# Three reorderings around PE's waits in a two-layer decoder trunk: key copies, memory products, one chunk's split

## The chip, the cores and the metric

The kernel runs on one core of one Trainium2 chip. The metric is the device time of one execution in microseconds (us); runs are compared by their median. PE is the matmul engine (PEld its weight loads), DVE the vector engine, ACT the scalar engine, POOL the GpSimd engine, and SP the engine whose queue issues most of the DMAs.

## The reference

A residual stream of 256 tokens of width 1024 passes two layers. Each layer has a token mixer with memory cross-attention beside it, a layer norm, a large product-key expert layer (PEER), and a second layer norm. Layer 0's mixer is an mLSTM, layer 1's an RG-LRU.

```
for i in range(2):
    z = x @ w_in[i]                                   # mixer streams and 4 cross-attention query heads
    hm = mlstm_mixer(z) if i == 0 else rglru_mixer(z)
    ha = cross_attention(xq, mem, xattn_w_kv[i])       # kv = mem @ w_kv; softmax over 256 memory tokens
    mix = concat([hm, ha]) @ w_out[i]
    x = layer_norm(ALPHA * x + mix, ln1_g[i], ln1_b[i])
    y = peer_ffn(x, peer_w_q[i], peer_subkeys[i], peer_u[i], peer_v[i])   # top 16 of 16384 experts, 8 heads
    x = layer_norm(ALPHA * x + y, ln2_g[i], ln2_b[i])
```

## The kernel before

Everything is computed in float32 quality with three matmuls for one product. A number is split into a high part, rounded to the fast matmul format (`wH`, `xH`, `memH`), and the remainder (`wL`, `xL`, `memL`); `mm3` (lines 182 to 186) multiplies high by high, high by low and low by high. Weights come from memory in chunks of 128 rows by up to 1024 columns. The program is written out by hand in one order for all engines, and each engine works off its own queue in that order.

**The ring of chunks.** `plan` lists every chunk in the order of use. `load` (L139) issues the DMA of a chunk on SP's queue into one of five buffers `raw`. `pump` splits it: a cast on ACT makes `wH` (L110), and a subtraction makes `wL`, either on DVE (L125), on POOL (L123), or with the first `pool_cols` columns on POOL and the rest on DVE. The rest can be put off (`put_off`): then it is kept in the list `owed` and issued later. A raw buffer is free when all readers are done. `next` hands out the next chunk; it pumps up to three chunks ahead (`HL_BUFS`), and first lets a side generator take a step.

**Side generators.** `beside(gen)` registers work that is issued in small steps, one step at each call of `next`. In layer 0's mixer, `gates` (L592) is such a generator: it computes the gates of the mLSTM on [4, 256] tiles on ACT and DVE, and copies the projected keys from PSUM into `kT` on ACT with `keys(t0, t1)` (L645). Its steps run while the projection of the queries goes on, whose chunks (`w0qx`) alternate with four parts of the transposed memory (`memT`, cast on ACT to `memH`, subtracted on POOL to `memL`).

**Layer norm.** `norm` (L284) is a generator that lets the caller issue matmuls at each of its `yield`s. It has two halves of tokens, tt = 0 and 1. `add` and `half` (L303 to L311) add the residual and take statistics, `stats` (L315, L316) finishes them, `center` (L324) and `spread` (L329) scale a stretch of 256 or 512 columns, `scale` does both, `scale_beside` (L336 to L340) does it on ACT and POOL. `turn(tt, q, n)` transposes a stretch of the result on PE (L350), casts it on ACT into `xH` (L354) and subtracts on DVE into `xL` (L355), the operands of the next projection. `idle` (L249) puts transposes of the identity into PE's queue.

- *Behind the token mixer* (`early`): `proj_n` with a `tail` calls it. In layer 0 the tail is 6 chunks, in layer 1 all 8 (`tail == DT`). After `g` and `b`, the norm's weights, the ring holds the first chunks of the query projection `w_q`. The norm pumps the first of them with its `wL` wholly on POOL, and the next, with 512 columns on POOL and 512 put off, between the first and second statistics of tt = 1. Later it scales the first two blocks of tt = 1 on DVE (L425), transposes them (L428), casts them (L429), subtracts (L432), issues what was put off, and scales the next quarter (`scale(1, 1, 1)`). The rest of the scaling and turning goes into the generator `rest`, which steps at each `next` of the following projection: `scale(0, 2, 2)` and `turn(1, 1, 1)`, then `scale(1, 2, 2)` and `turn(0, 2, 2)`, then `turn(1, 2, 2)`. That projection belongs to `peer_layer`, which first clears 16 small tiles on POOL (L1093, L1094).
- *Behind layer 0's experts* (`fill`): the caller passes a generator `memory` with six steps of products that do not depend on the norm, four of `mem_k` and two of `mem_v` (12 matmuls each), for the cross-attention of layer 1. The norm takes some of them before, between and after its turns, so that PE has work while DVE scales.

The steps of `memory` in the order before:

```
next(fill), next(fill)
turn(0, 0, 1), turn(1, 0, 1)
scale(0, 2, 2)
owed.pop()()
next(fill)
turn(0, 1, 1), turn(1, 1, 1)
scale(1, 2, 2)
next(fill), next(fill)
turn(0, 2, 2)
next(fill)
turn(1, 2, 2)
```

Of the kernel before, what the change touches and what calls it, by code (L numbers as in the profile page):

```python
# [19 lines left out]
D = 1024  # L20
T = 256
DT = 8
# [12 lines left out]
MIX_COLS = 0  # L35
# [15 lines left out]
class Trunk:  # L51
# [98 lines left out]
    def next(self, ahead=HL_BUFS):  # L150
        while callable(self.items[self.n_got][2]) or self.items[self.n_got][3] is not None:
            self.pump(self.n_got + 1)
            self.split.pop(self.n_got, None)
            self.n_got += 1
        i = self.n_got
        if self.ahead:
            next(self.ahead, None)
        self.pump(i + ahead)
        self.n_got += 1
        self.tick()  # L160
        return self.split.pop(i)
# [37 lines left out]
    def proj_n(self, splits, stat, order=range(DT), tail=0, extra=EXTRA, hook=(-1, None)):  # L199
        sH, sL = stat  # L200
        parts = [splits, (512, 256, 256) if tail else splits]
        banks = [[self.bank() for _ in p] for p in parts]
        late = []

        def products(tt, k, late):
            t = slice(tt * P, (tt + 1) * P)
            w = parts[tt][k]
            c0 = sum(parts[tt][:k])
            for n_, dt_, (h, l) in late:
                self.mm3(banks[tt][k][:, :w], sH[:, dt_, t], sL[:, dt_, t], h[:, c0:c0 + w], l[:, c0:c0 + w],  # L210
                         n_ == 0, n_ == last[tt])
        n_ring = DT - 2 - extra
        last = (DT - 1, DT - 1 - n_ring if tail else DT - 1)
        for n, dt in enumerate(order):
            if n == hook[0]:
                hook[1]()
            late.append((n, dt, self.next(min(HL_BUFS + min(n, extra), DT - n) if tail else HL_BUFS)))
            if n + 1 > DT - tail and n + 1 < DT:
                continue
            if tail and n + 1 == DT:  # L220
                break
            for tt in range(2):
                for k in range(len(parts[tt])):
                    products(tt, k, late)
            late = []
        if not tail:
            return banks
        ln = self.norm(banks, False, True)
        if tail == DT:
            own, ring = late[2:2 + extra], late[:2] + late[2 + extra:]  # L230
            parts0 = [[c] for c in late]
        else:
            parts0 = own, ring = late[:-n_ring], late[-n_ring:]
        for n, part in enumerate(parts0):
            if tail == DT and n == 2:
                self.idle(FILL[2])
            for k in range(2):
                products(0, k, part)
        next(ln)
        for k in range(3):  # L240
            products(1, k, ring)
        for k in range(3):
            products(1, k, own), next(ln, None)
# [37 lines left out]
        tmp.__exit__(None, None, None)  # L281


    def norm(self, y, last, early, fill=False):  # L284
        nc, x = self.nc, self.x
        alpha = 1.0 if last or fill else ALPHA
        fine = early or last
# [18 lines left out]
        def half(tt, q0, n):  # L306
            if fine and tt:
                for q in range(q0, q0 + n):
                    nc.vector.bn_stats(st[:, tt, q, :], x[:, tt, q * Q:(q + 1) * Q])
            else:  # L310
                nc.vector.bn_stats(st[:, tt, q0 // 2, :], x[:, tt, q0 * Q:(q0 + 2) * Q])  # L311
# [9 lines left out]
        def center(tt, q, n):  # L321
            qs = slice(q * Q, (q + n) * Q)
            xs = x[:, tt, qs]
            nc.vector.scalar_tensor_tensor(xs, xs, mv[:, tt, 0:1], g[:, qs], op0=ALU.subtract, op1=ALU.mult)  # L324
# [61 lines left out]
            part = add(1, 0)  # L386
        half(*part)
        owed = []
        if early:
            self.pool_cols = D  # L390
            self.pump(self.n_got + 3)
        self.pool_cols, self.put_off = 512, owed.append
        self.pump(self.n_got + 3 + early)
        self.put_off = None
        self.pool_cols = MIX_COLS
        yield
        half(*add(1, 1))
        yield
# [4 lines left out]
        if fill:  # L403
            center(1, 0, 1), root(1), spread(1, 0, 1)
            scale(1, 1, 1)
            next(fill), next(fill)
            turn(0, 0, 1), turn(1, 0, 1)
            scale(0, 2, 2)
            owed.pop()()
            next(fill)  # L410
            turn(0, 1, 1), turn(1, 1, 1)
            scale(1, 2, 2)
            next(fill), next(fill)
            turn(0, 2, 2)
            next(fill)
            turn(1, 2, 2)
            self.release("g", "b")
            yield
            return
# [10 lines left out]
        low()  # L430
        for dt in range(2):
            nc.vector.tensor_sub(self.xL[:, dt, P:], ps[dt][:, :P], self.xH[:, dt, P:].bitcast(F32))  # L432
        self.idle(FILL[1])
        owed.pop()()
        scale(1, 1, 1)
# [116 lines left out]
    def mlstm_layer(self):  # L552
        nc, tc, A = self.nc, self.tc, self.A
        with ExitStack() as ctx:
# [37 lines left out]
            def gates():  # L592
                ig, fg = g2[:, 0, :], g2[:, 1, :]
                ab, e, wv, ln, F, lf = (gt[:, i, :] for i in range(6))
                nc.scalar.activation(fg, kg[3][32:36, :T], AF.Identity, bias=bg[:, 1:2])
                nc.scalar.activation(ig, kg[3][0:4, :T], AF.Identity, bias=bg[:, 0:1])
                nc.vector.scalar_tensor_tensor(ab, fg, -1.0, fg, op0=ALU.mult, op1=ALU.min)
                nc.vector.scalar_tensor_tensor(ab6, lam, -1.0, lam, op0=ALU.mult, op1=ALU.min)
                keys(0, 1)
                yield  # L600
                nc.scalar.activation(e, ab, AF.Exp)
                nc.scalar.activation(e6, ab6, AF.Exp)
                nc.vector.tensor_scalar(wv, e, 1.0, None, op0=ALU.add)
                nc.vector.tensor_scalar(w6, e6, 1.0, None, op0=ALU.add)
                nc.vector.memset(ab, 1.0)
                keys(1, 2)
                yield
                nc.scalar.activation(ln, wv, AF.Ln)
                nc.scalar.activation(l6, w6, AF.Ln)
                nc.vector.scalar_tensor_tensor(wv, wv, -1.0, e, op0=ALU.add, op1=ALU.subtract)  # L610
                keys(2, 4)
                yield
                nc.vector.scalar_tensor_tensor(lf, fg, 0.0, ln, op0=ALU.min, op1=ALU.subtract)
                nc.vector.tensor_add(lf, lf, wv)
                keys(4, 6)
                yield
                nc.vector.tensor_tensor_scan(F, ab, lf, 0.0, op0=ALU.mult, op1=ALU.add)
                yield
                nc.vector.tensor_sub(rt[0:4, :], ig, F)
                nc.vector.tensor_tensor_scan(M, rt[0:4, :], rt[0:4, :], 0.0, op0=ALU.max, op1=ALU.max)  # L620
                yield
                nc.vector.tensor_add(ab, F, M)
                nc.vector.tensor_copy(rt[32:36, :], ab)
                nc.vector.tensor_scalar(M, M, -1.0, None, op0=ALU.mult)
                yield
                nc.scalar.dma_start(row, M)
                nc.vector.scalar_tensor_tensor(w6, w6, -1.0, e6, op0=ALU.add, op1=ALU.subtract)
                nc.vector.tensor_sub(l6, l6, w6)
                nc.vector.tensor_scalar(ab6, lam, -1.0, 0.0, op0=ALU.mult, op1=ALU.max)
                nc.vector.tensor_add(l6, ab6, l6)  # L630
                nc.vector.tensor_scalar(n8, l6, 8.0, None, op0=ALU.mult)
                nc.vector.tensor_scalar(c8, l6, -8.0, None, op0=ALU.mult)
                yield
                every = lambda n, o: bass.AP(tensor=row.tensor, offset=row.offset + o, ap=[[0, P], [T, 4], [1, n]])
                nc.scalar.dma_start(pw[:, :, 0:T], every(T, 0))
                nc.scalar.dma_start(pw[:, :, T:384], every(P, P))
                diag = bass.AP(tensor=pw.tensor, offset=pw.offset, ap=[pw.ap[0], [384, 4], [T, 2], [1, P]])
                nc.gpsimd.tensor_tensor(diag, diag, maskn.unsqueeze(1).unsqueeze(1).to_broadcast([P, 4, 2, P]),
                                        op=ALU.add)

            def keys(t0, t1):
                for tl in range(t0, t1):
                    src = kg[tl // 2][:, (tl % 2) * T:(tl % 2 + 1) * T]
                    for h, part, rows in KMAP[tl]:
                        nc.scalar.activation(kT[rows, h, part, :], src[rows], AF.Copy, scale=192.0 ** -0.5)  # L645
# [43 lines left out]
            for h in range(4):  # L689
                n = self.bank()  # L690
# [838 lines left out]
```

## Time and profile before

| | us |
|---|---|
| median of 3 runs | 1803.55 |
| lowest and highest | 1802.96 and 1803.71 |
| the profiled execution | 1803.17 |
| its span | 1801.4 |
| PE, DVE, ACT, POOL busy in it | 1785.8, 1489.8, 1012.4, 427.0 |

The span runs from the first to the last instruction of the profiled execution. All starts in the profile's rows are in us from the start of the span. A row of a timeline gives the start, the duration, engine, line, operation, result and operands with their sizes, how many instructions it stands for (xN), and in brackets the idle time ahead of it and what ended that. Matmuls overlap, so that a matmul of 0.28 us is followed by the next one much sooner. A row of waits names the waiting instruction, what released it, the total, the number of waits and the longest.

### The profile page before, as it was taken

Reading aid. Unit: us, or ns where it says so; the run is one execution under the profiler, and the core shown is the slowest. Engines: PE = TensorE matmul, PEld = TensorE weight load, DVE = VectorE, ACT = ScalarE, POOL = GpSimd, SP = SyncE. Lnnn points to the kernel's source line nnn. Section 1 sums busy time; section 2 is a strip of 40 time slices with the busy share of each in tenths; the row PEclk is TensorE's granted clock in tenths of the full one; section 3 lists DMA queues with packets and bytes.
Section 4 is the critical chain, followed back from the end, with each engine's and each line's share of the span. In section 5 each row is a group of like instructions: output and inputs, shape, how many; then the busy total and the mean of one; then the engine's idle time right before and its main releaser. Section 6 shows DMA issues by size and latency. Waiting matters only on the chain.

```text
span 1801.4 us, 33797 instructions
## 1 busy us (share of the span) xinstructions
PE 1785.8 (99%) x12717; PEld 1648.6 (92%) x12717; DVE 1489.8 (83%) x3091; ACT 1012.4 (56%) x1786; POOL 427.0 (24%) x324
## 2 busy tenths in 40 slices
PE   8999999999999999999999999999999999999998
PEld 8999999999999888888899899999999988888886
DVE  6674779599998899998867848685999989999987
ACT  6554555455554666665647355554555456666663
POOL 2015772333332000000101368325333300000000
PEclk9999999999999999999999999999999999999999
DMA  7656566655555566655755455665555556555664
GB/s 249 202 161 197 169 195 192 193 171 165 163 160 160 190 206 210 208 200 182 255 184 182 131 176 178 197 191 187 164 161 159 162 188 204 193 194 194 207 200 139
DMA packets 95557, 334.24 MB, mean 186 GB/s; under 512 B 10652, under 2 KB 13728, under 8 KB 95136
## 3 DMA queue, kind: packets, MB, share of 16 engines
q1 hardware_dynamic: 93752, 328.93, 56.7%
q10 hardware_dynamic: 1640, 3.15, 0.5%
q8 instruction: 99, 1.62, 0.4%
q14 instruction: 66, 0.54, 0.1%
HBM read 330.98 MB, written 1.05 MB: 184 GB/s over the span
## 4 chain that ended last, share of the span: by engine, by line
PE 74%; issue 16%; POOL 7%; DVE 2%; ACT 1%; DMA 0%; POOLq 0%; SPq 0%; DVEq 0%
PE bank L186 24%; PE bank L185 24%; PE bank L184 23%; POOL wL L120 7%; PE bank L256 3%; ACT wH L110 0%; DVE wL L125 0%; PE bank L350 0%; POOL wL L123 0%; PE bank L527 0%; DVE x L324 0%; PE bank L249 0%; DMA cp<-in_rg_par_dram 0%; DVE x L303 0%; DMA raw<-in_w0kg_dram 0%
## 5 line engine op out<-in xcount | busy, mean ns | idle before, releaser
L110 ACT CAST wH<-raw 128x1024 fp32r<-128x1024 f32 (+3 forms) x605 | 612.5, 1013 | 664.8 <-POOL wL L120 187.6
L184 PE MATMUL bank<-xHL,wH 128*128 128x256 f32 x2536 | 715.5, 282 | 4.6 <-ACT wH L110 4.6
L186 PE MATMUL bank<-xHL,wL 128*128 128x256 f32 x2536 | 702.5, 277 | 0.5 <-DVE wL L125 0.5
L185 PE MATMUL bank<-xHL,wH 128*128 128x256 f32 x2536 | 702.5, 277 | 0.0
L125 DVE TENSOR_TENSOR wL<-raw,wH 128x1024 fp32r<-128x1024 f32 (+3 forms) x413 | 449.5, 1090 | 227.3 <-ACT wH L110 226.4
L184 PEld LDWEIGHTS bank<-xHL,wH 128*128 128x128 f32 x2536 | 477.2, 188 | 4.7 <-ACT wH L110 4.6
L186 PEld LDWEIGHTS bank<-xHL,wL 128*128 128x128 f32 x2536 | 477.0, 188 | 1.1 <-DVE wL L125 0.7
L185 PEld LDWEIGHTS bank<-xHL,wH 128*128 128x128 f32 x2536 | 477.7, 188 | 0.1
L185 PE MATMUL bank<-wL,cH 128*128 128x512 f32 x850 | 331.1, 390 | 0.4 <-DVE wL L125 0.4
L186 PE MATMUL bank<-wH,cL 128*128 128x512 f32 x850 | 330.7, 389 | 0.0
L184 PE MATMUL bank<-wH,cH 128*128 128x512 f32 x850 | 330.3, 389 | 0.0
L123 POOL TENSOR_TENSOR wL<-raw,wH 128x1024 fp32r<-128x1024 f32 (+1 forms) x121 | 253.5, 2098 | 210.1 <-ACT wH L110 209.2
L120 POOL TENSOR_TENSOR wL<-raw,wH 128x386 fp32r<-128x386 f32 x126 | 129.5, 1028 | 280.1 <-DVE wL L118 280.1
L185 PEld LDWEIGHTS bank<-wL,cH 128*128 128x128 f32 x850 | 159.5, 188 | 34.8 <-DVE wL L125 1.3
L184 PEld LDWEIGHTS bank<-wH,cH 128*128 128x128 f32 x850 | 159.6, 188 | 33.7
L186 PEld LDWEIGHTS bank<-wH,cL 128*128 128x128 f32 x850 | 159.6, 188 | 33.6
L1036 DVE TENSOR_TENSOR oh<-iota,i12T 128x1024 f16<-128x1024 f16 x128 | 130.6, 1020 | 0.0
L339 POOL TENSOR_TENSOR x<-x,raw 128x256 f32<-128x256 f32 x6 | 5.0, 826 | 466.4 <-ACT x L336 466.4
L118 DVE TENSOR_TENSOR wL<-raw,wH 128x640 fp32r<-128x640 f32 x126 | 104.0, 825 | 7.5
L1039 DVE TENSOR_TENSOR oh<-oh,gT 128x1024 f16<-128x1024 f16 x128 | 90.1, 704 | 4.4
L1169 PE MATMUL bank<-oh 128*128 128x128 f16 x1024 | 80.9, 220 | 1.1 <-DVE oh L1039 1.1
L1169 PEld LDWEIGHTS <-oh 128*128 128x128 f16 x1024 | 58.8, 97 | 6.0 <-DVE oh L1039 1.5
(336 smaller groups left out, 2134.2 us busy)
## 6 DMA issues: line engine op xcount, KB each, us to landing
raw<-in_u_dram SPq DMA_DIRECT2D x256, 512.0 KB, 3.5
raw<-in_v_dram SPq DMA_DIRECT2D x256, 512.0 KB, 4.4
raw<-in_w_q_dram SPq DMA_DIRECT2D x32, 512.0 KB, 3.7
raw<-in_w_out_dram SPq DMA_DIRECT2D x16, 512.0 KB, 3.7
raw<-in_w0qx_dram SPq DMA_DIRECT2D x8, 512.0 KB, 5.1
raw<-in_wkv_dram SPq DMA_DIRECT2D x8, 512.0 KB, 5.1
raw<-in_w0v_dram SPq DMA_DIRECT2D x8, 384.0 KB, 5.0
raw<-in_w0o_dram SPq DMA_DIRECT2D x8, 384.0 KB, 3.0
```

Source lines behind the costliest of these rows:

```text
L110: (nc.vector.tensor_copy if self.cast_dve else nc.scalar.copy)(h[:, c], r[:, c])
L118: nc.vector.tensor_sub(l[:, k:], r[:, k:], h[:, k:].bitcast(F32))
L120: nc.gpsimd.tensor_sub(l[:, :k], r[:, :k], h[:, :k].bitcast(F32))
L123: nc.gpsimd.tensor_sub(l[:, :k], r[:, :k], h[:, :k].bitcast(F32))
L125: rest = lambda l=l, r=r, h=h, c=slice(k, n): nc.vector.tensor_sub(l[:, c], r[:, c], h[:, c].bitcast(F32))
L184: mm(out, sH, mH, start=start, stop=False, skip_group_check=True)
L185: mm(out, sH, mL, start=False, stop=False, skip_group_check=True)
L186: mm(out, sL, mH, start=False, stop=stop, skip_group_check=True)
L256: self.nc.tensor.matmul(out, lhsT, rhs, start=start, stop=stop, skip_group_check=True)
L1036: nc.vector.tensor_tensor(flat(oh[:, 1:3]), self.iota2.unsqueeze(1).to_broadcast([P, 4, P, 2]), pairs(self.i12T[:, j]), op=ALU.is_equal)
L1039: nc.vector.tensor_tensor(flat(oh[:, 0:2]), two.rearrange("p z (q e t) -> p z q e t", q=2, t=2), pairs(self.gT[:, j]), op=ALU.mult)
L1169: nc.tensor.matmul(wp[:, qs], oh[:, 2, q // 2, :, q % 2], oh[:, z, q // 2, :, q % 2], start=z == 0, stop=z == 1, skip_group_check=True)
```

## The change

Three moves, and no instruction more or less:

1. In `gates`, `keys(2, 4)` moves from the third step to the fourth, and `keys(4, 6)` from the fourth to the fifth. In ACT's queue each of the two groups of copies now stands one memory part and one weight chunk later.
2. In the norm behind layer 0's experts, three steps of `memory` come ahead of the first turns instead of two, and one fewer comes behind `scale(1, 2, 2)`. In PE's queue the third part of `mem_k` stands before the first four transposes, the fourth before the next four, and the first of `mem_v` alone before the four after them.
3. In layer 1's norm behind the mixer, the split of the second `w_q` chunk (the fourth item of the ring, counted with `g` and `b`) is issued behind the first casts and subtractions of tt = 1. In ACT's queue its cast moves from before the first turn to behind the L429 casts. In the queues of DVE and POOL the order stays: POOL's half still stands ahead of the 16 clears, DVE's half still behind L432. The three lines that set and reset `pool_cols` and `put_off` become a helper, `ahead`, for both norms behind a mixer.

```
-        ln = self.norm(banks, False, True)
+        ln = self.norm(banks, False, True, late=tail == DT)
...
-    def norm(self, y, last, early, fill=False):
+    def norm(self, y, last, early, fill=False, late=False):
...
         owed = []
+
+        def ahead(n, cols):
+            self.pool_cols, self.put_off = cols, owed.append
+            self.pump(self.n_got + n)
+            self.put_off = None
+            self.pool_cols = MIX_COLS
         if early:
-            self.pool_cols = D
-            self.pump(self.n_got + 3)
-        self.pool_cols, self.put_off = 512, owed.append
-        self.pump(self.n_got + 3 + early)
-        self.put_off = None
-        self.pool_cols = MIX_COLS
+            ahead(3, D)
+        if not late:
+            ahead(3 + early, 512)
         yield
...
-            next(fill), next(fill)
+            next(fill), next(fill), next(fill)
             turn(0, 0, 1), turn(1, 0, 1)
             scale(0, 2, 2)
             owed.pop()()
             next(fill)
             turn(0, 1, 1), turn(1, 1, 1)
             scale(1, 2, 2)
-            next(fill), next(fill)
+            next(fill)
             turn(0, 2, 2)
...
             nc.vector.tensor_sub(self.xL[:, dt, P:], ps[dt][:, :P], self.xH[:, dt, P:].bitcast(F32))
+        if late:
+            ahead(3 + early, 512)
         self.idle(FILL[1])
         owed.pop()()
         scale(1, 1, 1)
...
                 nc.vector.scalar_tensor_tensor(wv, wv, -1.0, e, op0=ALU.add, op1=ALU.subtract)
-                keys(2, 4)
                 yield
                 nc.vector.scalar_tensor_tensor(lf, fg, 0.0, ln, op0=ALU.min, op1=ALU.subtract)
                 nc.vector.tensor_add(lf, lf, wv)
-                keys(4, 6)
+                keys(2, 4)
                 yield
                 nc.vector.tensor_tensor_scan(F, ab, lf, 0.0, op0=ALU.mult, op1=ALU.add)
+                keys(4, 6)
                 yield
```

## The prediction

> **What bounds the kernel now.** I read the page first, then the waits of PE, then, around each place where PE waits, the timelines of PE, ACT, DVE and POOL, and last those same stretches by DVE and POOL alone.
>
> ```profile
> span 1801.4 us, 33797 instructions
> ...
> PE 1785.8 (99%) x12717; PEld 1648.6 (92%) x12717; DVE 1489.8 (83%) x3091; ACT 1012.4 (56%) x1786; POOL 427.0 (24%) x324
> ```
>
> The whole list of what PE waited for is short. Three of its rows carry this change (total, times, longest, in us):
>
> ```profile
> PE bank L428 <- DVE x L425: 0.9, 2, 0.7
> PE bank L350 <- DVE x L329: 0.5, 1, 0.5
> PE bank L186 <- DVE wL L125: 0.5, 1, 0.5
> ```
>
> PE is busy in 99% of the span, so an edit that moves only ACT, DVE or POOL work can pay or cost where PE waits for them and nowhere else. Each edit aims at one of these waits: the key copies at the L186 one, the memory products at the L350 one, the later split at the longer of the two L428 ones. No instruction is added or dropped; all three are changes of order. So what is at stake is under 2.5 us of 1801.4, and the question for each edit is what is late next.
>
> **Edit 1, key copies two steps later (layer 0).** PE, ACT, DVE and POOL around the wait (start, duration):
>
> ```profile
> 36.81 0.28 PE L184 MATMUL bank<-xHL,wH 128*128 128x256 f32 x1
> 36.92 0.28 PE L185 MATMUL bank<-xHL,wH 128*128 128x256 f32 x1
> 37.74 0.38 PE L186 MATMUL bank<-xHL,wL 128*128 128x256 f32 x1 [0.55 <-DVE wL L125]
> ...
> 40.65 0.38 PE L186 MATMUL bank<-xHL,wL 128*128 128x256 f32 x1
> ```
>
> ```profile
> 34.05 0.66 ACT L645 ACTIVATE kT<-bank 128x256 f32<-128x256 f32 x2
> 34.59 0.62 ACT L110 CAST memH<-raw 128x512 fp32r<-128x512 f32 x1
> 35.10 1.06 ACT L110 CAST wH<-raw 128x1024 fp32r<-128x1024 f32 x1
> 36.06 1.16 ACT L645 ACTIVATE kT<-bank 64x256 f32<-64x256 f32 x3
> ```
>
> ```profile
> 35.30 1.31 POOL L123 TENSOR_TENSOR memL<-raw,memH 128x512 fp32r<-128x512 f32 x1 [5.08 <-ACT memH L110]
> 37.80 3.96 POOL L123 TENSOR_TENSOR memL<-raw,memH 128x512 fp32r<-128x512 f32 x2 [1.20 <-ACT memH L110]
> ```
>
> ```profile
> 36.20 1.49 DVE L125 TENSOR_TENSOR wL<-raw,wH 128x1024 fp32r<-128x1024 f32 x1 [1.81 <-ACT wH L110]
> 39.39 1.21 DVE L125 TENSOR_TENSOR wL<-raw,wH 128x1024 fp32r<-128x1024 f32 x1
> ```
>
> PE's L186 starts at 37.74, just behind the end of the wL subtraction (36.20 + 1.49 = 37.69). Without the wait it would follow L185 by one pitch of 0.11 us (36.81 to 36.92), at 37.03, so 0.71 us are lost. The subtraction took 1.49 us where its neighbour took 1.21: it stood still until POOL's memL subtraction ended (35.30 + 1.31 = 36.61) and then ran 1.08 us.
>
> With the two copies moved behind this chunk, the memH cast starts at 34.05 instead of 34.59, and POOL's memL, the wH cast and what follows move by the same 0.54. POOL ends at 36.07, wL at 36.07 + 1.08 = 37.15, L186 starts at 37.20: 0.54 gained, 0.17 of the wait left. What is late next is the following chunk. On ACT the copies come behind wH (35.52 to 36.18), then memH and wH of that chunk, the second of them ending near 37.7; its memL subtraction on POOL waits for DVE until 37.15 and ends near 38.3; the two small gate operations of DVE queued behind wL wait for that and end near 39.0; then wL runs 1.21, to 40.2. PE gets to that chunk's L186 at 37.20 + (40.65 - 37.74) = 40.1 and waits about 0.1 more. It starts at 40.2 instead of 40.65. **Edit 1 is worth 0.45 us**, between 0.2 and 0.7 (the whole wait). The loads queued on SP behind these buffers are released earlier, not later. The moved copies read banks that nobody wants back in these steps.
>
> **Edit 2, one more part of memory products (layer 0's last norm).** PE, then DVE, then POOL:
>
> ```profile
> 918.06 0.38 PE L350 MATMUL bank<-ident,x 128*128 128x128 f32 x2
> 918.92 0.44 PE L350 MATMUL bank<-ident,x 128*128 128x128 f32 x2 [0.48 <-DVE x L329]
> ...
> 925.84 0.60 PE L350 MATMUL bank<-ident,x 128*128 128x128 f32 x4
> ```
>
> ```profile
> 918.11 0.76 DVE L329 SCALAR_TENSOR_TENSOR x<-x,rs,raw 128x256 f32<-128x256 f32 x1
> 918.79 1.50 DVE L324 SCALAR_TENSOR_TENSOR x<-x,mv,raw 128x256 f32<-128x256 f32 x1
> ...
> 924.89 0.75 DVE L329 SCALAR_TENSOR_TENSOR x<-x,rs,raw 128x512 f32<-128x512 f32 x1
> ```
>
> ```profile
> 918.54 1.46 POOL L123 TENSOR_TENSOR wL<-raw,wH 128x512 fp32r<-128x512 f32 x1
> ```
>
> The second pair of transposes waits 0.64 us (918.92 less 918.06 and two pitches of 0.11) for L329, which ends at 918.87. Twelve products at that pitch (1.3 us) put in front cover that wait wholly. But DVE's order does not change, and DVE runs from there without a pause to the last L329 of this norm, 924.89 + 0.75 = 925.64, on which the last four transposes depend; they started at 925.84. PE arrives there 0.64 us sooner, at 925.20, and waits until 925.69 (the earlier pair started 0.05 behind its L329). So the wait mostly moves to the last transposes: **edit 2 is worth 0.15 us**, between 0 and the 0.64 that it would be if DVE were not the next bound.
>
> **Edit 3, the fourth chunk's split behind the first copies (layer 1's first norm).** PE; then the same DVE instruction in layer 0's norm and in this one; then POOL; then ACT:
>
> ```profile
> 1016.83 0.50 PE L428 MATMUL bank<-ident,x 128*128 128x128 f32 x2 [0.75 <-DVE x L425]
> ...
> 1020.62 0.38 PE L350 MATMUL bank<-ident,x 128*128 128x128 f32 x2
> ...
> 1026.85 0.60 PE L350 MATMUL bank<-ident,x 128*128 128x128 f32 x4
> ```
>
> ```profile
> 136.93 0.48 DVE L324 SCALAR_TENSOR_TENSOR x<-x,mv,raw 128x256 f32<-128x256 f32 x1
> ```
>
> ```profile
> 1015.15 1.07 DVE L324 SCALAR_TENSOR_TENSOR x<-x,mv,raw 128x256 f32<-128x256 f32 x1
> ...
> 1018.98 1.51 DVE L329 SCALAR_TENSOR_TENSOR x<-x,rs,raw 128x256 f32<-128x256 f32 x1
> ...
> 1022.99 1.45 DVE L125 TENSOR_TENSOR wL<-raw,wH 128x512 fp32r<-128x512 f32 x1
> ...
> 1025.14 0.75 DVE L329 SCALAR_TENSOR_TENSOR x<-x,rs,raw 128x512 f32<-128x512 f32 x1
> ...
> 1029.06 0.69 DVE L125 TENSOR_TENSOR wL<-raw,wH 128x512 fp32r<-128x512 f32 x1 [0.26 <-ACT wH L110]
> ```
>
> ```profile
> 1012.31 3.63 POOL L123 TENSOR_TENSOR wL<-raw,wH 128x1024 fp32r<-128x1024 f32 x2
> 1015.88 0.20 POOL L1093 MEMSET edge<- 128x128 f16 x1
> ...
> 1018.93 1.28 POOL L123 TENSOR_TENSOR wL<-raw,wH 128x512 fp32r<-128x512 f32 x1 [0.65 <-ACT wH L110]
> ...
> 1029.10 1.80 POOL L123 TENSOR_TENSOR wL<-raw,wH 128x512 fp32r<-128x512 f32 x1 [1.89 <-ACT wH L110]
> ```
>
> ```profile
> 1017.16 0.47 ACT L429 CAST xHL<-bank 128x128 fp32r<-128x128 f32 x2 [1.72 <-PE bank L428]
> ...
> 1017.80 1.05 ACT L110 CAST wH<-raw 128x1024 fp32r<-128x1024 f32 x1 [0.17 <-ACT xHL L429]
> ...
> 1024.79 1.05 ACT L110 CAST wH<-raw 128x1024 fp32r<-128x1024 f32 x1
> ```
>
> Three rules of this kernel can be read off. A DVE instruction with two SBUF operands that meets a running POOL subtraction stands until that ends, and then needs 0.28 us for 256 columns (1018.93 + 1.28 = 1020.21, L329 ends 1020.49) or about 0.55 for 512 (L125 of 1022.99). A POOL subtraction that meets such a DVE instruction ends 1.15 us after it (1029.06 + 0.69 = 1029.75, POOL ends 1030.90). And where POOL already waits, it goes before the next DVE instruction: in edit 2's rows POOL (918.54) ends 1.15 behind L329 and the L324 queued at 918.79 takes 1.50.
>
> The Trainium skill, SBUF — State Buffer, section "SBUF: two separate sides", describes this as an exclusive lock on a port pair that DVE and GpSimd share: whichever starts first has it for the whole instruction and the other blocks fully. The trace agrees: 1.07 us against 0.48 for the same L324.
>
> *The gain.* The fourth chunk's POOL half (the second of the 1012.31 pair, to 1015.94) holds up L324 by 0.59 us. Moved away, L324, L425, L428 and the copies all come 0.59 sooner.
>
> *The price.* The moved split still has to be done. Its wH cast stands on ACT right behind the L429 copies (ending 1017.63 - 0.59 = 1017.04), so wH is there at 1018.1. Then DVE's and POOL's halves start together: DVE to 1018.8, POOL to 1018.8 + 1.15 = 1019.9. Behind it on DVE stands the scale of the next quarter, L324 and L329: L324 ends 1019.9 + 0.28 = 1020.2, L329 at 1020.7. The pair of transposes at 1020.62 wants that at 1020.03 now; it starts at 1020.75. The 0.59 is gone, and 0.15 with it.
>
> POOL, which takes its queue in order, does the 16 memsets only now. They took 1015.88 to 1018.28 (the 0.65 of idle ahead of 1018.93), 2.4 us, so they run to 1022.25, and the next subtraction, which started at 1018.93, starts there, as DVE begins the 512-column L329. From here POOL catches up with one subtraction behind the other, and DVE gets one instruction in between each time. DVE first: that L329 ends 1022.95, POOL 1024.1, DVE's L125 1024.65, POOL's third subtraction 1025.8, L324 of the last half 1026.35. The next wH cast, at 1024.79 before, is at 1024.95 and done at 1026.0, so POOL's fourth subtraction is waiting when L324 ends, goes first, ends 1027.5, and the last L329 ends 1028.05 (before: 1025.14 + 0.75 = 1025.89). The last transposes start at 1028.1 instead of 1026.85. POOL first gives the same within 0.1. **Edit 3 costs 1.25 us**; the ends are a gain of 0.59 (none of these meetings happens) and a loss of 1.5 (a fifth meeting of 0.28). I take 1.25, since the rules come from rows of this very stage.
>
> **Sum.** -0.45 - 0.15 + 1.25 = +0.65 us on the profiled execution, which took 1803.17 us (span 1801.4 and 1.8 around it): 1803.8. The median of the runs, 1803.55, stands 0.38 above that execution, so the forecast is 1804.2. A measurement of this kernel tells about 0.2%, 3.6 us, from no change; this is far inside.
>
> **The rivals.**
>
> *No pile-up (20%).* DVE slips in ahead of POOL, edit 3 keeps its 0.59: -0.45 - 0.15 - 0.59 = -1.2, 1802.4. For it: the meetings hang on starts less than 0.1 us apart. Against it: the 1.80 of POOL stands at the chunk behind this stage too (1029.10), so meeting halves are the normal case.
>
> *A short pile-up (15%).* POOL's fourth subtraction comes behind the last L329; then edit 3 costs 0.15 to 0.4, about 0.3: net -0.3, 1803.25. It decides at 1026.35: wH would have to end later than that, 0.35 us later than I work out.
>
> *All three waits simply go (5%).* 0.71 + 0.64 + 0.75 = 2.1 us: 1801.45. Against it stand DVE's unbroken run to 925.64 and the moved subtraction.
>
> *Slower: POOL's fourth memL goes before the next wL in edit 1 (7%).* Its memH cast now stands behind the three copies of 1.16 us and ends near 39.2, after DVE has begun that wL near 38.95. If the cast ended before that, POOL would go first, wL would end 1.15 later, and edit 1 would lose 0.7 instead of gaining 0.45: total +1.8, 1805.35. The point is 0.25 us away.
>
> **How the numbers follow.** My forecast has 53%; its own range is 1803.4 to 1804.9 (edit 1 from 0.2 to 0.7, edit 3 up to 1.5, and 0.4 for the spread of the runs). The range of 8 in 10 takes in the short pile-up and most of no pile-up: 1802.0 to 1805.1; it leaves out the last two rivals and the edges. Every case lies within 3.6 us of 1803.55, so "within 0.2%" gets 0.95; faster and slower keep 0.02 and 0.03 for a cause that no row here shows.
>
> **What would show it.** Right: PE's wait at L186 near 37 shrinks to some 0.2 and a second one of that size stands near 40; the wait of the L350 pair at 918 is gone and one of about 0.5 stands before the last four of that norm; L324 at 1015 takes 0.48; and two new PE waits stand in front of transposes, some 0.7 near 1020 and some 1.1 near 1027, with POOL subtractions end to end. Wrong: L329 before the last transposes of layer 1 ends by 1025.5, or wL near 40 ends later than before.

## The result and the profile after

| kernel | median of its runs | lowest to highest | profiled execution | its span |
|---|---|---|---|---|
| before | 1803.47 us (22 runs beside the changed kernel) | 1802.69 to 1804.38 | 1803.17 us | 1801.4 us |
| after | 1807.55 us (22 runs) | 1805.41 to 1808.88 | 1808.21 us | 1806.4 us |

The change makes the kernel slower: ratio 1.0021, interval 1.0015 to 1.0026, or 4.1 us between the medians. The forecast was 1804.2 with a range up to 1805.1, so the result lies outside it. The 22 runs fall into two groups: 7 from 1805.41 to 1806.76 us, in all of which the granted clock over the whole span was 0.999, and 15 from 1807.05 to 1808.88, at 0.998. That third decimal turns out to be part of the effect: in this kernel every execution at 0.998 is longer than every one at 0.999, while a single one at 0.998, as some others below have it, is not longer than its neighbours. One execution of the kernel before (1828.2 us at a granted clock of 0.948) among the runs beside the last two experiments widens their intervals.

The page after, span and first row of busy times:

```profile
span 1806.4 us, 33796 instructions
...
PE 1788.9 (99%) x12717; PEld 1651.2 (91%) x12717; DVE 1491.5 (83%) x3091; ACT 1012.3 (56%) x1786; POOL 427.7 (24%) x324
```

PE is busy for 3.1 us longer (1788.9 against 1785.8) with the same 12717 matmuls: some matmuls themselves took longer. The list of what PE waited for (total, times, longest, in us):

```profile
PE bank L184 <- ACT wH L110: 4.5, 1, 4.5
PE bank L350 <- DVE x L329: 3.7, 3, 2.7
...
PE bank L431 <- DVE x L428: 0.3, 2, 0.2
```

The L186 wait is off the list, and the wait of the first transposes of tt = 1, those whose copies follow at L429 (L428 before, L431 now), fell from 0.9 to 0.3. But L350 went from 0.5 to 3.7, with one single wait of 2.7. (The edit shifts lines: L425, L428, L429 and L432 of before are L428, L431, L432 and L435 now; the 16 clears are L1098 and L1099.)

**Edit 1.** PE, then DVE, near 37 and 40 us:

```profile
37.50 0.28 PE L184 MATMUL bank<-xHL,wH 128*128 128x256 f32 x1
37.78 0.39 PE L186 MATMUL bank<-xHL,wL 128*128 128x256 f32 x1
...
40.48 0.28 PE L184 MATMUL bank<-xHL,wH 128*128 128x256 f32 x1
40.81 0.39 PE L186 MATMUL bank<-xHL,wL 128*128 128x256 f32 x1
```

```profile
36.24 1.48 DVE L125 TENSOR_TENSOR wL<-raw,wH 128x1024 fp32r<-128x1024 f32 x1 [1.15 <-ACT wH L110]
...
39.55 1.21 DVE L125 TENSOR_TENSOR wL<-raw,wH 128x1024 fp32r<-128x1024 f32 x1
```

From L184 to L186 there are two pitches, 0.23 us. L186 starts 0.28 and 0.33 behind L184, so 0.05 and 0.10 us are lost where 0.71 and 0.07 were. PE came to this place 0.69 us later than before (its L184 at 37.50 instead of 36.81); that is the start of the kernel, which other runs below shift as well, without this edit too. The wait did not go because PE was late: in e2 and e3 below, which leave edit 1 out, PE is late as well and the 0.7 us stand.

**Edit 2.** The last L329 of layer 0's last norm, and the last four transposes:

```profile
924.83 0.75 DVE L329 SCALAR_TENSOR_TENSOR x<-x,rs,raw 128x512 f32<-128x512 f32 x1
925.64 0.66 PE L350 MATMUL bank<-ident,x 128*128 128x128 f32 x4 [0.53 <-DVE x L329]
```

No wait is left near 918, and PE waits 0.69 us here instead, where it did not wait before. The transposes start at 925.64, not 925.84.

**Edit 3.** First DVE, then POOL, then PE in layer 1's first norm:

```profile
1015.01 0.49 DVE L324 SCALAR_TENSOR_TENSOR x<-x,mv,raw 128x256 f32<-128x256 f32 x1
...
1018.49 1.52 DVE L324 SCALAR_TENSOR_TENSOR x<-x,mv,raw 128x256 f32<-128x256 f32 x1
1020.04 0.48 DVE L329 SCALAR_TENSOR_TENSOR x<-x,rs,raw 128x256 f32<-128x256 f32 x1
1020.45 1.78 DVE L1094 COPY iotac<-iota 128x256 f16<-128x256 f16 x1
1022.15 1.77 DVE L125 TENSOR_TENSOR wL<-raw,wH 128x512 fp32r<-128x512 f32 x1
1023.84 1.75 DVE L324 SCALAR_TENSOR_TENSOR x<-x,mv,raw 128x512 f32<-128x512 f32 x1
1025.62 0.75 DVE L329 SCALAR_TENSOR_TENSOR x<-x,rs,raw 128x512 f32<-128x512 f32 x1
```

```profile
1017.93 1.80 POOL L123 TENSOR_TENSOR wL<-raw,wH 128x512 fp32r<-128x512 f32 x1 [3.40 <-ACT wH L110]
1019.67 0.20 POOL L1098 MEMSET edge<- 128x128 f16 x1
...
1021.87 0.21 POOL L1099 MEMSET wide<- 128x128 f16 x1
1022.04 3.00 POOL L123 TENSOR_TENSOR wL<-raw,wH 128x512 fp32r<-128x512 f32 x2
```

```profile
1016.10 0.50 PE L431 MATMUL bank<-ident,x 128*128 128x128 f32 x2 [0.16 <-DVE x L428]
1020.58 0.44 PE L350 MATMUL bank<-ident,x 128*128 128x128 f32 x2 [0.52 <-DVE x L329]
1026.42 0.66 PE L350 MATMUL bank<-ident,x 128*128 128x128 f32 x4 [2.66 <-DVE x L329]
```

The DVE row to look at is the fourth, the copy of `iota` into `iotac`. In before it stood in the same place of DVE's queue, behind the L329 of this quarter, and was over in 0.28 us, as this row of before shows:

```profile
1020.41 0.28 DVE L1089 COPY iotac<-iota 128x256 f16<-128x256 f16 x1
```

Now it runs 1.78 us. It starts while POOL does its clears (1019.67 to 1022.08) and ends at 1022.23, 0.15 us behind them. Behind it L125 meets one POOL subtraction and L324 the next, 1.77 and 1.75 us, and PE, which has done its last matmul ahead of these transposes at 1023.49 plus one pitch, stands until 1026.42.

Then the clock. The windows of after, of which the columns that matter are PE busy (the second value behind the window) and PEclk (the seventh):

```profile
core 0: us, PE busy (x) PEld busy (x) DVE busy (x) ACT busy (x) POOL busy (x), PEclk, DMA share, GB/s
...
1024.00:1026.00 2.00, 0.00 (x0) 0.00 (x0) 1.96 (x2) 0.00 (x0) 1.04 (x1) 1.00 0.41 125
1026.00:1028.00 2.00, 1.57 (x13) 1.58 (x14) 1.97 (x4) 0.88 (x2) 0.00 (x0) 0.95 0.34 137
1028.00:1030.00 2.00, 2.00 (x11) 2.00 (x10) 2.00 (x3) 0.65 (x1) 1.27 (x1) 0.50 0.75 223
1030.00:1032.00 2.00, 2.00 (x14) 2.00 (x14) 0.55 (x1) 0.11 (x1) 0.01 (x1) 0.70 0.85 342
1032.00:1034.00 2.00, 2.00 (x19) 2.00 (x19) 1.23 (x2) 1.43 (x2) 0.50 (x1) 1.00 0.97 379
```

```profile
1027.38 0.28 PE L185 MATMUL bank<-xHL,wH 128*128 128x256 f32 x1
1027.50 0.28 PE L186 MATMUL bank<-xHL,wL 128*128 128x256 f32 x1
...
1029.15 0.41 PE L186 MATMUL bank<-xHL,wL 128*128 128x256 f32 x1
1029.36 0.41 PE L184 MATMUL bank<-xHL,wH 128*128 128x256 f32 x1
```

After the long wait PE works at full pitch (0.12 us) for a good microsecond, and then, from about 1027.8 to 1031.1, at 0.21: the granted clock is 0.50 from 1027.80 to 1031.21. These are the longer matmuls that the busy row pointed to.

### The profile page after: what moved, and what is told of

It reads as the page before. It is cut to its first block, busy times and chain, and to the rows that moved or that the text cites. A ratio compares the mean times of both kernels' runs of the same rounds, so it can differ in the third digit from the quotient of the medians.

```text
span 1806.4 us, 33796 instructions
## 1 busy us (share of the span) xinstructions
PE 1788.9 (99%) x12717; PEld 1651.2 (91%) x12717; DVE 1491.5 (83%) x3091; ACT 1012.3 (56%) x1786; POOL 427.7 (24%) x324
## 3 DMA queue, kind: packets, MB, share of 16 engines
q8 instruction: 99, 1.62, 0.4%
## 4 chain that ended last, share of the span: by engine, by line
PE 74%; issue 16%; POOL 7%; DVE 2%; ACT 0%; DMA 0%; POOLq 0%; DVEq 0%; SPq 0%; ACTq 0%
PE bank L186 24%; PE bank L185 24%; PE bank L184 24%; POOL wL L120 7%; PE bank L256 3%; DVE x L324 0%; ACT wH L110 0%; DVE wL L125 0%; DVE x L329 0%; POOL wL L123 0%; PE bank L532 0%; PE bank L350 0%; DVE x L303 0%; DMA raw<-in_w0kg_dram 0%; PE bank L249 0%
## 5 line engine op out<-in xcount | busy, mean ns | idle before, releaser
L110 ACT CAST wH<-raw 128x1024 fp32r<-128x1024 f32 (+3 forms) x605 | 612.2, 1013 | 661.6 <-POOL wL L120 187.5
L184 PE MATMUL bank<-xHL,wH 128*128 128x256 f32 x2536 | 716.7, 283 | 4.5 <-ACT wH L110 4.5
L186 PE MATMUL bank<-xHL,wL 128*128 128x256 f32 x2536 | 703.7, 277 | 0.0
L125 DVE TENSOR_TENSOR wL<-raw,wH 128x1024 fp32r<-128x1024 f32 (+3 forms) x413 | 449.2, 1090 | 227.0 <-ACT wH L110 226.3
L184 PEld LDWEIGHTS bank<-xHL,wH 128*128 128x128 f32 x2536 | 478.5, 189 | 4.5 <-ACT wH L110 4.5
L186 PEld LDWEIGHTS bank<-xHL,wL 128*128 128x128 f32 x2536 | 478.2, 189 | 0.5 <-DVE wL L115 0.2
L186 PE MATMUL bank<-wH,cL 128*128 128x512 f32 x850 | 330.7, 389 | 0.0
L184 PE MATMUL bank<-wH,cH 128*128 128x512 f32 x850 | 330.2, 389 | 0.0
L184 PEld LDWEIGHTS bank<-wH,cH 128*128 128x128 f32 x850 | 159.6, 188 | 33.7
L186 PEld LDWEIGHTS bank<-wH,cL 128*128 128x128 f32 x850 | 159.6, 188 | 33.5
```

Source lines behind the costliest of these rows:

```text
L110: (nc.vector.tensor_copy if self.cast_dve else nc.scalar.copy)(h[:, c], r[:, c])
L125: rest = lambda l=l, r=r, h=h, c=slice(k, n): nc.vector.tensor_sub(l[:, c], r[:, c], h[:, c].bitcast(F32))
L184: mm(out, sH, mH, start=start, stop=False, skip_group_check=True)
L186: mm(out, sL, mH, start=False, stop=stop, skip_group_check=True)
```

## The experiments

To compare traces I cut each at the starts of two groups of four L350 transposes in layer 1's first norm: the ones near 1013 us, before anything of edit 3, and those that wait 2.66 us after the change. "Head" ends at the first and holds the start of the kernel and edits 1 and 2, "middle" runs between them, "tail" from the second to the end of the span. PE's transposes in this norm are, in order: four of L350 near 1013, the two of L431 (the first copies of tt = 1 hang on them), two of L350 near 1020 (called the first later ones), four (the second group) and four (the last).

| trace | head | middle | tail | median of runs | ratio to before, interval |
|---|---|---|---|---|---|
| before | 1013.73 | 9.94 | 777.73 | | |
| after | 1013.60 | 12.82 | 779.98 | 1807.55 | 1.0021 [1.0015, 1.0026] |
| e1: edit 1 alone | 1014.46 | 9.85 | 777.99 | 1803.21 | 0.9997 [0.9988, 1.0006] |
| e2: edit 2 alone | 1015.07 | 9.94 | 777.79 | 1803.93 | 1.0000 [0.9991, 1.0009] |
| e3: edit 3 alone | 1014.47 | 12.81 | 777.82 | 1808.25 | 1.0022 [1.0013, 1.0031] |
| e4: edits 1 and 2 | 1014.55 | 9.83 | 778.02 | 1803.35 | 0.9998 [0.9989, 1.0007] |
| e5: after, iotac copy on ACT | 1013.97 | 10.01 | 778.82 | 1804.52 | 1.0007 [0.9998, 1.0016] |
| e6: after, clears later | 1013.34 | 10.89 | 777.77 | 1804.04 | 1.0004 [0.9995, 1.0013] |
| e7: after, PE kept busy | 1013.73 | 12.93 | 777.74 | 1805.88 | 1.0013 [1.0004, 1.0022] |
| e8: after, split on DVE, scale first | 1013.02 | 9.99 | 777.79 | 1803.44 | 1.0000 [0.9991, 1.0009] |
| e9: e8, clears and copy later | 1013.46 | 9.92 | 777.92 | 1803.39 | 0.9989 [0.9967, 1.0012] |
| e10: e4, clears and copy later | 1013.18 | 9.80 | 777.92 | 1803.32 | 0.9989 [0.9967, 1.0012] |

The kernel before stood at a median of 1803.74 beside e1 to e4, 1803.4 beside e5 to e8 and 1803.64 beside e9 and e10. Heads spread over 2 us from trace to trace; those of e1 to e4, which ran together, are the highest whatever the edit. Middles and tails repeat within some 0.3 where nothing was changed in them. So the middle and the tail can be read to tenths, the total cannot.

**Which edit.** e1 and e2 are the kernel before with one edit each, e3 has the third alone, e4 the first two.

```
e1:  gates: keys(2, 4) and keys(4, 6) one step later each; rest as before
e2:  norm(fill): next(fill) three times ahead of the first turns, once behind scale(1, 2, 2); rest as before
e3:  after, with keys and next(fill) as before
e4:  after, with
-        ln = self.norm(banks, False, True, late=tail == DT)
+        ln = self.norm(banks, False, True, late=False)
```

> The kernel before with the first edit alone (the key copies two steps later). Theory (the loss is wholly in the third edit): PE's wait at L186 near 37 us falls from 0.71 to below 0.2, one of about 0.1 stands near 40.6; 0.3 to 0.6 us faster than before, so 0.9997 to 0.9998 of it; no other place changes. Rival (the first 34 us, where the changed kernel ran 0.7 us later, are made later by this edit): 0.1 to 0.7 us slower than before.

> The kernel before with the second edit alone (one more part of memory products ahead of the first turns). Theory: the wait of 0.64 us at 918 turns up as one of 0.6 to 0.7 in front of the last four transposes near 925, since DVE's own chain ends there; 0.0 to 0.2 us faster. Rival (the wait goes): 0.64 us faster, no wait near 925.

> The kernel before with the third edit alone (the fourth chunk's split behind the first casts). Theory: the whole loss is here. 4.3 to 5.3 us slower than before, 1.0024 to 1.0029; the waits of PE are some 0.3 at the first copies, 0.7 at the next transposes and 2.8 at the ones after, with the granted clock at about 0.5 for some 3 us behind that in most executions. Rival (the three edits share the loss): under 3 us slower.

> The changed kernel with the third edit taken back, that is the first and second edits together. Theory: 0.4 to 0.8 us faster than before (0.9996 to 0.9998), and 4.5 to 5 us faster than the changed kernel; the granted clock stays at 1.00 everywhere. Rival (the first two edits carry part of the loss): slower than before.

The loss is edit 3's, whole: 1808.25 alone, against 1803.35 for the other two together. In e1 0.04 us are lost near 37 and 0.17 near 40 (0.71 and 0.07 before): 0.57 less, which cannot be seen in the total, since the heads spread by more. In e2 the wait near 918 is gone and one of 0.72 us stands before the last transposes.

e3's profiled execution has the long wait but not the slow clock, as two of its windows show:

```profile
1026.00:1028.00 2.00, 0.72 (x6) 0.72 (x7) 1.97 (x4) 0.03 (x1) 0.00 (x0) 1.00 0.64 246
1028.00:1030.00 2.00, 2.00 (x20) 2.00 (x19) 1.97 (x4) 1.51 (x2) 0.42 (x1) 1.00 0.31 66
```

That makes it the measure of both parts. Its middle is that of after (12.81 and 12.82, 2.87 over before), and its tail is 2.16 us shorter: the waits cost 2.9 us, the clock 2.2 where it drops. Its 11 runs fall into the same two groups: three at 1806.50 to 1806.87 us with 0.999, eight at 1807.53 to 1808.78 with 0.998. The lower group stands 2.8 to 3.1 above before, close to the middle's 2.9.

**What stretches the copy, and what makes the wait.** e5 takes the iotac copy off DVE, e6 leaves it and takes the clears away from it:

```
e5:
-                nc.vector.tensor_copy(self.iotac, self.iota2[:, :16, 0:1].to_broadcast([P, 16, 16]))
+                nc.scalar.copy(self.iotac, self.iota2[:, :16, 0:1].to_broadcast([P, 16, 16]))
e6:  the two lines that clear edge and wide, from the start of peer_layer to behind
     the first eight chunks of w_q
```

> The changed kernel with one copy moved from DVE to ACT: the small f16 constant iotac that the expert layer makes at its start, which took 0.28 us in the kernel before and 1.78 in the changed one, where it runs into POOL's 16 clears. Theory (the clears hold DVE's copy, and the two POOL subtractions behind them come before DVE's scaling): without it the wait of 2.8 us before the second group of transposes goes, and the one of about 1.1 us that the prediction had before the last group comes back; the one of 0.7 us stays; no drop of the granted clock; 0.3 to 1.2 us slower than before. Rival (POOL's delay of the second chunk alone makes the long wait): the 2.8 us stay and so does the time of the changed kernel.

> The changed kernel with the 16 clears on POOL issued behind the first eight chunks of the expert layer instead of ahead of them, in both layers. Theory: the iotac copy takes 0.28 us again; but two POOL subtractions now stand directly behind each other, so that the wait before the first later transposes grows from 0.7 to about 1.6 us and the 2.8 us wait goes; no drop of the granted clock; within 0.5 us of before, most likely 0.3 slower. Rival (the clears do not matter): as slow as the changed kernel.

Either is enough to remove the long wait. e6's POOL and DVE:

```profile
1017.67 3.21 POOL L123 TENSOR_TENSOR wL<-raw,wH 128x512 fp32r<-128x512 f32 x2 [3.38 <-ACT wH L110]
...
1019.79 1.37 DVE L329 SCALAR_TENSOR_TENSOR x<-x,rs,raw 128x256 f32<-128x256 f32 x1
1021.08 0.28 DVE L1094 COPY iotac<-iota 128x256 f16<-128x256 f16 x1
```

With no clear running, the copy takes its 0.28 us again. But POOL's second subtraction now follows the first at once, L329 meets it (1.37 us), and PE waits 1.66 us at the first later transposes: the middle is 0.95 over before. In e5 DVE has no copy in its queue, and PE's groups, then three of DVE's instructions, stand like this:

```profile
1020.97 0.44 PE L350 MATMUL bank<-ident,x 128*128 128x128 f32 x2 [0.63 <-DVE x L329]
...
1023.98 0.60 PE L350 MATMUL bank<-ident,x 128*128 128x128 f32 x4
1028.21 0.63 PE L350 MATMUL bank<-ident,x 128*128 128x128 f32 x4 [0.81 <-DVE x L329]
```

```profile
1022.21 0.75 DVE L329 SCALAR_TENSOR_TENSOR x<-x,rs,raw 128x512 f32<-128x512 f32 x1
...
1024.58 1.78 DVE L324 SCALAR_TENSOR_TENSOR x<-x,mv,raw 128x512 f32<-128x512 f32 x1
1026.40 1.67 DVE L329 SCALAR_TENSOR_TENSOR x<-x,rs,raw 128x512 f32<-128x512 f32 x1
```

This is the picture that the prediction drew for the changed kernel: 0.79 us lost at the first later transposes, none at the second group, 0.97 at the last. The three DVE instructions end at 1022.96, 1026.36 and 1028.07; the prediction had 1022.95, 1026.35 and 1028.05 (this trace reaches the norm 0.24 us later than before's). Its middle and tail are together 1.16 us over before; the forecast for edit 3 was 1.25.

**What slows the clock.** e7 leaves everything late and puts 22 transposes of the identity where PE stood idle:

```
             self.release("g", "b")
+            if late:
+                self.idle(22)
             turn(0, 2, 2)
```

> The changed kernel with 22 transposes of the identity (2.4 us of PE work that nobody reads) in front of the second group of transposes of that norm, where PE waits 2.8 us. Theory (PE's idle time makes the granted clock fall to a half for some 3 us in most executions): the wait shrinks to about 0.4 us, nothing that others wait for moves, the granted clock stays at 1.00, and the time is that of the fastest executions of the changed kernel, 2.3 to 3 us slower than before. Rival (the slow stretch behind the wait has another cause, or the fillers delay the transposes): as slow as the changed kernel or slower, 4 us and more.

```profile
1023.75 2.56 PE L249 MATMUL bank<-ident 128*128 128x128 f32 x22
1026.66 0.63 PE L350 MATMUL bank<-ident,x 128*128 128x128 f32 x4 [0.35 <-DVE x L329]
```

The fillers take 2.56 us of the wait, and 0.51 us of it are left; the middle, 12.93, is as long as after's. The tail is that of before, 777.74 against 777.73, and all 11 runs lie between 1805.33 and 1807.12, none in the group of 1807.5 to 1808.9 that held 8 of 11 runs of e3. The same late DVE with a PE that is not idle costs no clock: it is PE's own idleness that brings the drop.

Why the drop comes in some executions and not in others can be read from the kept traces. In after's trace the clock goes to 1.00 at 10.62 us, near the start of the kernel, and to 0.50 at 1027.80, 1017.17 us later; the half clock lasts 3.413 us, and 1017.17 is 298 times that. In e3's trace it rises at 9.08 and falls only behind the last matmul, at 1801.07: 1792.0 us, 525 times 3.413 (in the other traces it is 524 or 525 times). So the clock changes at marks 3.413 us apart, whose place in the kernel differs from execution to execution. Counted on from the rise, the stretches between marks around the long wait are these, two of after and then two of e3:

```profile
1024.38:1027.80 3.42, 1.38 (x12) 1.38 (x13) 3.38 (x5) 0.68 (x2) 0.66 (x1) 1.00 0.44 153
1027.80:1031.21 3.41, 3.41 (x18) 3.41 (x18) 2.72 (x4) 0.85 (x1) 1.28 (x1) 0.50 0.81 281
```

```profile
1022.84:1026.25 3.41, 1.79 (x16) 1.59 (x15) 3.41 (x3) 0.41 (x1) 3.05 (x3) 1.00 0.35 89
1026.25:1029.66 3.41, 2.38 (x21) 2.38 (x22) 3.34 (x7) 1.53 (x2) 0.08 (x1) 1.00 0.48 159
```

In after one stretch holds 2.04 us in which PE stands idle, and the clock drops at its end. In e3 a mark splits the same wait into 1.62 and 1.03 us, and the clock stays. If the idle time within one stretch decides, as these traces suggest, the limit lies between 1.62 and 2.04 us. An estimate checks this: marks that fall by chance leave more than 2.04 us of an idle time of 2.66 us in one stretch in 58% of cases, and more than 1.62 us in 83%; the drop came in 23 of the 33 executions of after and e3, 70%. No run sets the place of the marks or searches the limit.

**Can the late split pay.** e8 puts the moved split wholly on DVE and behind the scaling that PE waits for; e9 also moves the copy and the clears behind the first eight chunks. e10 is the control for e9, with the split where it was.

```
e8:
         if late:
-            ahead(3 + early, 512)
+            ahead(3 + early, 0)
         self.idle(FILL[1])
+        if late:
+            scale(1, 1, 1)
         owed.pop()()
-        scale(1, 1, 1)
+        if not late:
+            scale(1, 1, 1)
e9:   e8,  the iotac copy and the clears moved to where e6 has the clears
e10:  e4,  the same move
```

> The changed kernel with the moved split done wholly on DVE, none of it on POOL, and the scale of the next quarter ahead of it on DVE. Theory (it is the moved POOL half, before the scale on DVE and the clears on POOL, that costs): the third edit keeps its gain, the wait at the first copies stays at 0.3 us, no wait over 0.3 us stands at the later transposes of that norm; 1.0 to 1.6 us faster than before. Rival (any split at that place holds the projection up, since its chunk comes 1 us later): a wait of PE for this chunk's wL or for the next scale, and no faster than before.

> The kernel with the moved split wholly on DVE and the scaling of x(1,1,1) ahead of it, and now with the iotac copy and the 16 clears moved behind the first eight w_q chunks, so that neither lies between the norm's DVE instructions. Theory (what still cost time in that kernel was the iotac copy of 1.38 us in DVE's queue ahead of L324): without it L324 and L329 for turn(0,2,2) end near 1021.4 instead of 1022.95, PE's wait of 0.79 us at 1022.1 goes, no wait over 0.4 is left from 1015 to 1030, and the time is 0.5 to 0.9 us under the kernel before: 1802.5 to 1802.9 if that stands at 1803.4. Rival (POOL's chunks of the weights hold the DVE scaling whatever stands ahead of it): L329 takes 1.5 us or more again, a wait of 0.5 us or more comes before turn(0,2,2) or turn(1,2,2), and the time is that of the kernel before within 0.3 us.

> The control: edits 1 and 2 with the split where it was, and the iotac copy and the 16 clears moved as in the other kernel of this pair. If the late split is worth its 0.59 us once the pile-up is gone, this kernel keeps L324 at 1.07 us and its wait near 1016.6 (0.9 us) and stands 0.4 to 0.8 us above the other. If the moved copy and clears are what gains, the two stand alike, both under the kernel before by 0.3 us or more.

e8 takes the 0.59 us at the first copies and the wait at 1020 is gone, but one of 0.79 us comes before the second group of transposes at 1023.01, and the time is that of before, not the 1.0 to 1.6 us less that I expected. I put this wait on the copy (1.38 us there, beside a POOL subtraction). e9 says no: the copy is away, and POOL and DVE still meet.

```profile
1021.49 1.29 POOL L123 TENSOR_TENSOR wL<-raw,wH 128x512 fp32r<-128x512 f32 x1 [1.21 <-ACT wH L110]
1021.53 1.80 DVE L329 SCALAR_TENSOR_TENSOR x<-x,rs,raw 128x512 f32<-128x512 f32 x1
```

POOL starts 0.04 us ahead of L329, and the wait is 0.74. So the rival that I had beside it holds: POOL's next subtraction stands in the way with the copy ahead of it and without. e8 and e9 come out with the same middle as before (9.99 and 9.92 against 9.94), and e10, without the late split, at 9.80; nor does e10 stand above e9 in time (1803.32 against 1803.39), as it would if the late split kept its 0.59 us. No kernel here shows a gain that its interval could carry, and none is a version that beats the kernel before.

## Why the prediction was wrong

| part | forecast | what the traces show |
|---|---|---|
| edit 1 | -0.45 us | -0.62: 0.71 + 0.07 lost before, 0.05 + 0.10 after |
| edit 2 | -0.15 | -0.1: the same 88 matmuls take from 915.23 to 926.19 before (10.96 us), from 915.19 to 926.06 after (10.87); the wait itself moved, 0.64 to 0.69 |
| edit 3, waits | +1.25 | +2.9 (middle of e3 less middle of before) |
| edit 3, clock | no term | +2.2 in the executions where it drops, 0 in the others |

The parts add up to 2.2 us without the drop and 4.4 with it. The medians of the two groups of 7 and 15 runs, 1806.0 and 1808.1, stand 2.5 and 4.6 us above before.

*Edits 1 and 2* went by their steps. The next chunk's wait grew to 0.10, as forecast; the rival in which POOL goes ahead of the next wL did not come, as that wL took its 1.21. DVE's last L329 bounds layer 0's last norm at 925.6, where the prediction had it.

*Edit 3, the steps that held.* L324 at 1015 takes 0.49, and PE gets the 0.59 us at the first copies (0.91 lost before, 0.32 after). DVE's and POOL's halves of the moved split meet; POOL's takes 1.80, L324 behind it 1.52, and PE's wait at the first later transposes is 0.69 us (forecast: some 0.7). The clears end at 1022.1 (forecast: 1022.25), and POOL's subtractions do follow one another, with DVE instructions of 1.75 and 1.77 between.

*The step that failed* is the sentence ahead of "From here POOL catches up": it has POOL's next subtraction start "as DVE begins the 512-column L329". In the trace DVE was not there yet. The 16 clears were costed as POOL time alone, and what stands on DVE between the scaled quarter and that L329 was never listed: the 1.5 us of before (1020.49 to 1021.99) were kept (1020.7 to 1022.2), with the iotac copy in them, which before took 0.28 us in a place where POOL did no clears. Moving POOL's queue later moved the clears onto that copy, and it took 1.50 us longer, where the prediction has no wait. From then on DVE was late by more than one instruction: the L329 that the prediction had end at 1022.95, clear of POOL, began only at 1025.62, behind an L125 and an L324 that each met a subtraction, and the pile-up came ahead of the second group of transposes (2.83 us) where the prediction had some 1.1 us ahead of the last. e5 measures this step by itself: with only the copy gone, the rest of the working gives 1.16 us where it forecast 1.25.

The Trainium skill, SBUF — State Buffer, section "Who interferes with whom", bears on just this step: there, a DVE instruction with two SBUF inputs contends with a GpSimd instruction that reads SBUF and not with one that only writes, while for a copy in a two-port mode, which copies can enter, it makes no such exception. The traces agree with both halves, though none names the mode of a copy. L329 ran 0.48 us in the midst of the clears (1020.04), and the copy right behind it ended 0.15 us behind the last of them. The prediction had used another section of that page for the subtractions and did not ask which of DVE's other instructions the clears could hold.

*The missing term* is the clock. After pauses of 0.69 and 2.83 us, PE's clock was granted at 0.50 for 3.41 us. In the trace of after, 15 matmuls came at 0.21 instead of 0.11 us, about 1.6 of the 2.16 us; the rest is a pitch of 0.12 instead of 0.11 for some time behind. The Trainium skill, TensorE: Matmul & The Clock Gate, section "What's actually happening", gives the clock to a free-running window of about 3.4 us: after an idle window it falls to half. The half clock, its length, and that the same 2.8 us of waiting had it in after's trace and not in e3's agree with a window whose place varies. That a window be wholly idle does not: the stretch that ended with the drop held 2.04 us of idle time out of 3.41, and most executions dropped (15 of 22, and 8 of 11 in e3, by their times and the 0.998 of the whole run). Here the measurement decides.

The chances followed from the same gap. Every rival stayed within 3.6 us of before because each was made of waits alone; edit 3's waits with a drop behind them reach 5.1 us, and the result, 4.1, is past that line.

## What to carry to other kernels

When a queue is shifted, hold everything that stands on the neighbouring queues in the shifted stretch against it, also the short instructions that have nothing to do with the change: a 0.28 us copy became 1.78 us because clears slid under it. Where two engines hold each other up, as DVE and POOL do here, moving a chunk can move the meeting and not remove it: the late split in five settings (after, e5, e6, e8, e9) gave a wait at one or two of three places each time, and the best of them came out even. Price a long wait of TensorE above its own length: the one of 2.8 us took another 2.2 us of half clock here in 23 of 33 executions, and filler work in the gap took that part away.

## What was not expected of the hardware

- Clears of 128x128 f16 on POOL (0.15 us apart) hold an f16 copy of 128x256 on DVE until the last of the 16 is done, 1.78 us instead of 0.28, and leave a DVE instruction with two f32 operands of 128x256 alone, 0.48 us.
- The granted clock fell not in the wait but 1.4 us after PE took up work again (PE from 1026.42, pitch 0.21 from about 1027.8), and stayed at half for 3.41 us: at a mark 298 times 3.413 us behind the first rise of the clock, with 2.04 us of idle time in the stretch before it.
- A wait of 1.66 us (e6) showed no drop in its trace: its tail is 777.77, before's 777.73. Nor did the 2.8 us of e3's trace, of which the fuller stretch held 1.62 us of idle time.
